# Hybrid encoder block on one Trainium2 core: the first loads in pieces by two queues, idle products ahead of them, and a last store by a second queue

## The chip, the cores and the metric

The kernel runs on one core of one Trainium2 chip. The time is that of one execution in device microseconds; the runs' median is compared. The engines are named as in the profile: PE (TensorE, products; PEld its weight loads), DVE (VectorE), ACT (ScalarE), POOL (GpSimd) and SP (SyncE, which here only issues DMAs). Each engine works through its own list of instructions in order.

## The reference

One layer of a streaming encoder for 512 frames of width 1024, with a memory of 256 frames: RWKV-7 time mixing and an RG-LRU branch side by side, merged by gates, then cross-attention into the memory, then a gated convolutional FFN, each with an RMS norm ahead of it, and a last RMS norm. The change touches the start of the key projection of the memory, which the kernel does first, and the stores of the last norm.

```python
def rms_norm(x, g):
    xf = x.astype(jnp.float32)
    y = xf * lax.rsqrt(jnp.mean(xf * xf, axis=-1, keepdims=True) + NORM_EPS)
    return (y * g.astype(jnp.float32)).astype(x.dtype)

def cross_attention(h, m, w_q, w_kv, w_o):
    ...
    kv = m @ w_kv
    k = kv[..., :D_MODEL].reshape(bsz, -1, X_HEADS, X_HEAD_DIM)
    ...

# in reference():
        x = x + cross_attention(rms_norm(x, norm_x_g[l]), rms_norm(mem, norm_mem_g[l]),
                                w_cq[l], w_ckv[l], w_co[l])
        x = x + conv_ffn(rms_norm(x, norm_ffn_g[l]), w_ffn_in[l], ffn_conv_w[l],
                         ffn_conv_b[l], w_ffn_out[l])
    return rms_norm(x, norm_final_g)
```

## The kernel before

Products keep nearly the precision of float32 by a split: each operand is cut into a rounded part (`hi`, cast by ACT) and the rest (`lo`, a subtraction on DVE), and `mm3` makes three products: hi by hi, hi by lo, lo by hi. So each weight block of 128 by 1024 goes through a load by SP (`wk_r`, L102; four buffers), a cast on ACT (`wk_h`, L114; three buffers), a subtraction on DVE (`wk_l`, L115; three buffers) and 24 products on PE (L160 to L162). `stream` yields these blocks, and `Units` hands them out in eight units of 128 columns.

The first stage computes the keys of the memory, `k_ps`: eight weight blocks `wk`, each by all of the memory. The memory comes as `mraw`, in four quarters of 256 KB (`load_m`), each quarter two of the eight blocks of channels. Each channel block is scaled by the norm's gains and split: `m`, the rounded part on ACT (L281) and the rest on DVE (L282). The gains are 8 of the 240 columns of `pv`, a table of all parameters, loaded in one piece by ACT's queue. Apart from this ACT squares the memory (L284, L286) and DVE adds the squares into `mss` (L287); PE sums `mss` over partitions by a product with `ones` (`rs_ps`, L252, and `rmc_ps`, L294), and from that comes the norm's factor, which multiplies the keys when they leave PSUM (L306). After the keys come the values (`v_ps`), then the input projection (`in_ps`), and all the rest.

The first block of `wk` is loaded in two halves, and `un.fill` puts the loads of the quarters of the memory between them, on SP's queue:

```python
        nc.scalar.dma_start(pv, pv_d)
        load_m(0)
        un = Units(wk_d, "wk")
        un.fill(lambda i: [load_m(q) for q in ((1,), (2, 3))[i]])
```

A scheduler sets the order of the instructions on each engine when the program is built. Calls in `tc.keep_in_program_order` keep the order in which they are written, on their engine; those in `tc.high_priority()` go ahead of others; the rest goes where the scheduler expects it to be ready. Semaphores guard every buffer that is used again.

At the end the last rows of the FFN's output (`fol_ps`) are made in two halves of 256 frames. The second half is normed in two steps of 128 frames. In each step DVE multiplies (L1181) and SP stores (L1183) four channel blocks at a time, two stores of 256 KB a step.

Of the kernel before, what the change touches and what calls it, by code (L numbers as in the profile page):

```python
# [9 lines left out]
F32 = mybir.dt.float32  # L10
F32R = mybir.dt.float32r
AF = mybir.ActivationFunctionType
ALU = mybir.AluOpType
# [4 lines left out]
P = 128  # L18
# [12 lines left out]
IN_RWKV = [12, 13, 4, 5, 0, 1, 8, 9, 6, 7, 2, 3, 10, 11]  # L31
IN_REST = [22, 23, 24, 25, 26, 27, 28, 29, 30, 31, 32, 33, 34, 35, 36, 37, 14, 15, 16, 17, 18, 19, 20, 21]
NEARLY = 3
IN_ORDER = IN_RWKV + IN_REST


# [17 lines left out]
def hybrid_block_kernel(ctx: ExitStack, tc: tile.TileContext, xT_d, mT_d, pv_d, cst_d, win_d, wk_d, wv_d,  # L54
# [18 lines left out]
    def rw_ps(name, pool=None, tag="rw", **kw):  # L73
        return (pool or prw).tile([P, T], F32, tag=tag, name=name, **kw)
# [9 lines left out]
    def par(name, i, n=1):  # L84
        o = PV[name][0]
        return pv[:, o + i:o + i + n]
# [8 lines left out]
    def stream(dram, name, between=None, order=None):  # L95

        for g in order or range(dram.shape[0]):
            with tc.high_priority():
                raw = wp.tile([P, 1024], F32, tag="wr", name=f"{name}_r{g}", bufs=4)
                n = 1024 if between is None else 512  # L100
                for o in range(0, 1024, n):
                    ins = nc.sync.dma_start(raw[:, o:o + n], dram[g, :, o:o + n])  # L102
                    if between is not None:
                        tc.keep_in_program_order(ins)
                        between(o // n)
                    elif len(wdma) == 1:
                        tc.add_manual_dep(ins.ins, wdma[0].ins.name, mybir.DependencyInfo(
                            mybir.DependencyClass.NoSync, mybir.DependencyReason.DATA), reason="order of the loads")
                between = None
                wdma.append(ins)  # L110
                hi = wp.tile([P, 1024], F32R, tag="wh", name=f"{name}_h{g}")
                lo = wp.tile([P, 1024], F32R, tag="wl", name=f"{name}_l{g}")
                for o in range(0, 1024, n):
                    S.copy(hi[:, o:o + n], raw[:, o:o + n])  # L114
                    V.tensor_tensor(lo[:, o:o + n], raw[:, o:o + n], hi[:, o:o + n].bitcast(F32), ALU.subtract)  # L115
            yield hi, lo

    def stream_quarters(srcs, name):
# [81 lines left out]
    def ln_exp_set():  # L200

        return tc.keep_in_program_order(S.preload_act_table_set("natural_log_exp_and_others"))
# [57 lines left out]
    h2 = Split("hT2")  # L260

    with tc.tile_pool(name="p0", bufs=1, reuse_waits="tile") as p0:
        ln_exp_set()
        mraw = p0.tile([P, KB, NMEM], F32, name="mraw")
        xraw = p0.tile([P, KB, T], F32, name="xraw")

        def load_m(q):
            with tc.high_priority():
                tc.keep_in_program_order(
                    nc.sync.dma_start(mraw[:, 2 * q:2 * q + 2, :], mT_d[:, 2 * q:2 * q + 2, :]))  # L270

        nc.scalar.dma_start(pv, pv_d)
        load_m(0)
        un = Units(wk_d, "wk")
        un.fill(lambda i: [load_m(q) for q in ((1,), (2, 3))[i]])
        m2 = p0.tile([P, 2, KB, NMEM], F32R, name="m2")
        mss = p0.tile([P, NMEM], F32, name="mss")
        msq = [p0.tile([P, NMEM], F32, tag="msq", name=f"msq{k}", bufs=2) for k in range(KB)]
        for k in range(KB):
            g = par("nmem", k)  # L280
            S.activation(m2[:, 0, k, :], mraw[:, k, :], AF.Identity, scale=g)  # L281
            V.scalar_tensor_tensor(m2[:, 1, k, :], mraw[:, k, :], g, m2[:, 0, k, :].bitcast(F32),  # L282
                                   ALU.mult, ALU.subtract)
        S.activation(mss, mraw[:, 0, :], AF.Square)  # L284
        for k in range(1, KB):
            S.activation(msq[k], mraw[:, k, :], AF.Square)  # L286
# [878 lines left out]
    for hf in range(2):  # L1165
        ts = slice(hf * 256, (hf + 1) * 256)
        ps = pf.tile([P, T], F32, tag="x", name=f"fol_ps{hf}", bufs=4)
        for kb in range(FB):
            mm3(ps[:, :256], last[kb][0], last[kb][1], g2[kb][:, 0, ts], g2[kb][:, 1, ts], kb == 0, kb == FB - 1)
        step = 128 if hf else 256  # L1170
        for o in range(0, 256, step):
            ts = slice(hf * 256 + o, hf * 256 + o + step)
            sq = ffn_out(ps, KB - 1, ts, slice(o, o + step))
            pss = rw_ps(f"rs_ps{ts.start}", pf, "yz", bufs=4)
            PE.matmul(pss[:, :step], ones, sso[:, ts], start=True, stop=False)
            PE.matmul(pss[:, :step], ones, sq, start=False, stop=True)
            rsqrt(ro[:, ts], pss[:, :step], 1.0 / D, eps[:, 0:1], load=False)
            nb = 4 if hf else 2
            for m in range(0, KB, nb):
                ms = slice(m, m + nb)  # L1180
                V.tensor_tensor(xr[:, ms, ts], xr[:, ms, ts],  # L1181
                                ro[:, ts].unsqueeze(1).to_broadcast([P, nb, step]), ALU.mult)
                nc.sync.dma_start(out_d[:, ms, ts], xr[:, ms, ts])  # L1183


# [75 lines left out]
```

## Time and profile before

| | us |
|---|---|
| runs: all three | 942.82, 942.68, 939.07 |
| median of the runs | 942.68 |
| the profiled execution's own time | 939.86 |
| its span, from the first to the last instruction | 938.1 |
| PE busy | 917.7 (98% of the span) |
| DVE, ACT, POOL busy | 638.2, 468.9, 87.9 |

Times in the profile count from the start of the span. A row of the timeline has the start, the duration, the engine, the line, the operation, the output and inputs with their sizes, and in brackets how long the engine had been idle and what released it. `SPq` and `ACTq` are the issues of DMAs. Two rows of one engine that follow each other closely overlap a little, since the engines are pipelined: what one more instruction costs is read from start to start.

### The profile page before, as it was taken

Reading aid. Unit: us, or ns where it says so; the run is one execution under the profiler, and the core shown is the slowest. Engines: PE = TensorE matmul, PEld = TensorE weight load, DVE = VectorE, ACT = ScalarE, POOL = GpSimd, SP = SyncE. Lnnn points to the kernel's source line nnn. Section 1 sums busy time; section 2 is a strip of 40 time slices with the busy share of each in tenths; the row PEclk is TensorE's granted clock in tenths of the full one; section 3 lists DMA queues with packets and bytes.
Section 4 is the critical chain, followed back from the end, with each engine's and each line's share of the span. In section 5 each row is a group of like instructions: output and inputs, shape, how many; then the busy total and the mean of one; then the engine's idle time right before and its main releaser. Section 6 shows DMA issues by size and latency. Waiting matters only on the chain.

```text
span 938.1 us, 14783 instructions
## 1 busy us (share of the span) xinstructions
PE 917.7 (98%) x5856; PEld 770.4 (82%) x5856; DVE 638.2 (68%) x1043; ACT 468.9 (50%) x711; POOL 87.9 (9%) x101
## 2 busy tenths in 40 slices
PE   7999999999999999999999999999999999999996
PEld 6878776788877767788887778999999999888886
DVE  7784687668845768775566578788878878833333
ACT  7664655522235276434453466666546566532222
POOL 0102121000012200001111111112100000000000
PEclk9999999999999999999999999999999999999998
DMA  8869786464599922658886768999996656422202
GB/s 278 292 242 236 190 214 155 124 162 141 162 228 191 192 40 70 222 175 223 215 234 149 172 140 197 265 267 284 271 270 208 186 183 186 149 90 89 90 23 90
DMA packets 87813, 171.16 MB, mean 182 GB/s; under 512 B 23552, under 2 KB 28800, under 8 KB 87744
## 3 DMA queue, kind: packets, MB, share of 16 engines
q1 hardware_dynamic: 61728, 111.10, 37.7%
q0 software_dynamic: 18688, 47.19, 24.7%
q10 hardware_dynamic: 7328, 11.92, 3.8%
q8 instruction: 46, 0.75, 0.3%
q14 instruction: 23, 0.19, 0.1%
HBM read 158.92 MB, written 57.41 MB: 231 GB/s over the span
## 4 chain that ended last, share of the span: by engine, by line
PE 54%; DMA 3%; DVE 2%; ACT 2%; issue 1%; DVEq 0%; ACTq 0%
PE fo_ps L160 4%; PE fo_ps L161 4%; PE fo_ps L162 4%; PE fx_ps L160 4%; PE fx_ps L161 4%; PE fx_ps L162 4%; PE fyz_ps L161 3%; PE fyz_ps L160 3%; PE fyz_ps L162 3%; DMA wfi_r<-dS 2%; PE co_ps L161 2%; PE q_ps L161 2%; PE mix_ps L162 2%; PE mix_ps L160 2%; PE mix_ps L161 2%; PE q_ps L160 2%
## 5 line engine op out<-in xcount | busy, mean ns | idle before, releaser
L161 PE MATMUL in_ps<-hT,win_h 128*128 128x512 f32 x304 | 124.3, 410 | 0.0
L162 PE MATMUL in_ps<-hT,win_l 128*128 128x512 f32 x304 | 123.0, 405 | 0.0
L160 PE MATMUL in_ps<-hT,win_h 128*128 128x512 f32 x304 | 122.4, 404 | 0.0
L126 ACT CAST wfi_h<-wfi_r 128x1024 fp32r<-128x1024 f32 x77 | 81.0, 1051 | 81.4 <-PE fyz_ps L161 20.7
L127 DVE TENSOR_TENSOR wfi_l<-wfi_r,wfi_h 128x1024 fp32r<-128x1024 f32 x77 | 94.1, 1222 | 38.9 <-ACT wfi_h L126 38.7
L420 POOL DMA_DIRECT2D dS<-in_wfi x66 | 66.6, 1039 | 450.1 <-PE in_ps L160 172.1
L114 ACT CAST win_h<-win_r 128x1024 fp32r<-128x1024 f32 x38 | 39.9, 1049 | 86.7 <-PE in_ps L161 82.4
L115 DVE TENSOR_TENSOR win_l<-win_r,win_h 128x1024 fp32r<-128x1024 f32 x38 | 46.4, 1222 | 49.8 <-ACT win_h L114 49.0
L161 PEld LDWEIGHTS in_ps<-hT,win_h 128*128 128x128 f32 x304 | 57.3, 188 | 16.0 <-issue 2.2
L162 PEld LDWEIGHTS in_ps<-hT,win_l 128*128 128x128 f32 x304 | 57.3, 188 | 15.5 <-issue 2.0
L160 PEld LDWEIGHTS in_ps<-hT,win_h 128*128 128x128 f32 x304 | 57.1, 188 | 15.3 <-issue 1.4
L115 DVE TENSOR_TENSOR wfo_l<-wfo_r,wfo_h 128x1024 fp32r<-128x1024 f32 x22 | 26.9, 1225 | 52.1 <-ACT wfo_h L114 52.1
L114 ACT CAST wfo_h<-wfo_r 128x1024 fp32r<-128x1024 f32 x22 | 23.1, 1049 | 62.0 <-PE fo_ps L161 61.3
L160 PE MATMUL fx_ps<-hq,wfi_h 128*128 128x256 f32 x176 | 50.0, 284 | 2.1 <-ACT sn L1093 2.0
L161 PE MATMUL fx_ps<-hr,wfi_h 128*128 128x256 f32 x176 | 49.7, 282 | 0.0
L162 PE MATMUL fx_ps<-hr,wfi_l 128*128 128x256 f32 x176 | 49.6, 282 | 0.0
L160 PE MATMUL fx_ps<-hr,wfi_h 128*128 128x256 f32 x176 | 49.5, 281 | 0.0
L160 PE MATMUL fyz_ps<-hq,wfi_h 128*128 128x256 f32 x176 | 49.2, 280 | 0.0
L161 PE MATMUL fx_ps<-hq,wfi_h 128*128 128x256 f32 x176 | 49.2, 279 | 0.0
L161 PE MATMUL fyz_ps<-hq,wfi_h 128*128 128x256 f32 x176 | 49.1, 279 | 0.0
L162 PE MATMUL fx_ps<-hq,wfi_l 128*128 128x256 f32 x176 | 49.1, 279 | 0.0
L162 PE MATMUL fyz_ps<-hq,wfi_l 128*128 128x256 f32 x176 | 49.1, 279 | 0.0
(421 smaller groups left out, 2513.7 us busy)
## 6 DMA issues: line engine op xcount, KB each, us to landing
dS<-in_wfi POOLq DMA_DIRECT2D x66, 512.0 KB, 8.2
wfi_r<-dS SPq DMA_DIRECT2D x44, 512.0 KB, 6.4
win_r<-in_win SPq DMA_DIRECT2D x38, 512.0 KB, 4.7
wfi_r<-in_wfi SPq DMA_DIRECT2D x33, 512.0 KB, 5.3
dS<-dS POOLq DMA_DIRECT2D x22, 512.0 KB, 5.8
wfo_r<-in_wfo SPq DMA_DIRECT2D x22, 512.0 KB, 3.5
wv_r<-in_wv SPq DMA_DIRECT2D x8, 512.0 KB, 5.3
dG<-gs ACTq DMA_DIRECT2D x16, 256.0 KB, 2.1
```

The lines of the kernel that those rows point to most:

```text
L114: S.copy(hi[:, o:o + n], raw[:, o:o + n])
L115: V.tensor_tensor(lo[:, o:o + n], raw[:, o:o + n], hi[:, o:o + n].bitcast(F32), ALU.subtract)
L126: S.copy(hi, raw)
L127: V.tensor_tensor(lo, raw, hi.bitcast(F32), ALU.subtract)
L160: first = PE.matmul(ps, lh, rh, start=start, stop=False, **kw)
L161: PE.matmul(ps, lh, rl, start=False, stop=False, **kw)
L162: PE.matmul(ps, ll, rh, start=False, stop=stop, **kw)
L420: return lambda: nc.gpsimd.dma_start(s(out), src, **kw)
```

## The change

In the first stage: the first block of `wk` is loaded in four pieces of 256 columns instead of two of 512; the first quarter of the memory stays on SP's queue, and the other three go to ACT's, behind a load of the 8 columns of gains; the rest of `pv` is loaded by two more issues on ACT, kept in order behind the last copy of the memory. ACT's table load stands behind its first four issues. The casts, copies and subtractions of the first block and of the memory are kept in a written order (piece, two channel blocks, piece, two channel blocks, and so on). Nine products of `ones` by `ones` into a PSUM tile that nobody reads (`wake`) go first on PE. At the end, the last of the four stores of the last half goes to ACT's queue.

```diff
+NWAKE = 9
...
-                n = 1024 if between is None else 512
+                n = 1024 if between is None else 256
                 for o in range(0, 1024, n):
                     ins = nc.sync.dma_start(raw[:, o:o + n], dram[g, :, o:o + n])
                     if between is not None:
                         tc.keep_in_program_order(ins)
-                        between(o // n)
...
-                    S.copy(hi[:, o:o + n], raw[:, o:o + n])
-                    V.tensor_tensor(lo[:, o:o + n], raw[:, o:o + n], hi[:, o:o + n].bitcast(F32), ALU.subtract)
+                    a = S.copy(hi[:, o:o + n], raw[:, o:o + n])
+                    b = V.tensor_tensor(lo[:, o:o + n], raw[:, o:o + n], hi[:, o:o + n].bitcast(F32), ALU.subtract)
+                    if between is not None:
+                        tc.keep_in_program_order(a)
+                        tc.keep_in_program_order(b)
+                        between(o // n)
+                between = None
...
+        o, w = PV["nmem"]
+        with tc.high_priority():
+            tc.keep_in_program_order(nc.scalar.dma_start(pv[:, o:o + w], pv_d[:, o:o + w]))
+
         def load_m(q):
             with tc.high_priority():
+                tc.keep_in_program_order((nc.scalar if q else nc.sync).dma_start(
+                    mraw[:, 2 * q:2 * q + 2, :], mT_d[:, 2 * q:2 * q + 2, :]))
+
+        for q in range(KB // 2):
+            load_m(q)
+        ln_exp_set()
+        m2 = p0.tile([P, 2, KB, NMEM], F32R, name="m2")
+
+        def split_m(q):
+            for k in (2 * q, 2 * q + 1):
+                g = par("nmem", k)
                 tc.keep_in_program_order(
-                    nc.sync.dma_start(mraw[:, 2 * q:2 * q + 2, :], mT_d[:, 2 * q:2 * q + 2, :]))
-
-        nc.scalar.dma_start(pv, pv_d)
-        load_m(0)
+                    S.activation(m2[:, 0, k, :], mraw[:, k, :], AF.Identity, scale=g))
+                tc.keep_in_program_order(
+                    V.scalar_tensor_tensor(m2[:, 1, k, :], mraw[:, k, :], g, m2[:, 0, k, :].bitcast(F32),
+                                           ALU.mult, ALU.subtract))
+
         un = Units(wk_d, "wk")
-        un.fill(lambda i: [load_m(q) for q in ((1,), (2, 3))[i]])
+        un.fill(split_m)
+        for sl in (slice(0, o), slice(o + w, NPV)):
+            tc.keep_in_program_order(nc.scalar.dma_start(pv[:, sl], pv_d[:, sl]))
+        wake = rw_ps("wake")
+        with tc.high_priority():
+            for i in range(NWAKE):
+                PE.matmul(wake[:, 0:P], ones, ones, start=True, stop=True)
...
+        queues = [nc.sync, nc.scalar]
...
-                nc.sync.dma_start(out_d[:, ms, ts], xr[:, ms, ts])
+                q = queues[m // nb % 2] if ts.stop == T else nc.sync
+                q.dma_start(out_d[:, ms, ts], xr[:, ms, ts])
```

The scheduler orders the first stage anew; from the input projection on the order is the same but for that last store. Three places in the built programs matter. In the names the numbers are those of buffers; the weight blocks one to six are, before, `wk_r` 97, 202, 236, 270, 304 and 339, and now 101, 220, 254, 288, 322 and 357.

First, ACT's list from its start. Before:

```order
L202 ACT_TABLE_LOAD
L272 DMA pv<-in_pv 128x240
L284 ACTIVATE mss<-mraw 128x256
L286 ACTIVATE msq_112<-mraw 128x256
L114 CAST wk_h_103<-wk_r_97 128x512
L281 ACTIVATE m_109<-mraw,pv 128x256 x3
L114 CAST wk_h_103<-wk_r_97 128x512
L281 ACTIVATE m_109<-mraw,pv 128x256 x3
L286 ACTIVATE msq_113<-mraw 128x256
L286 ACTIVATE msq_114<-mraw 128x256
L114 CAST wk_h_204<-wk_r_202 128x1024
```

Now, from its fourth row on (the rows ahead are the four issues and the table load):

```order
L113 CAST wk_h_106<-wk_r_101 128x256
L289 ACTIVATE m_100<-mraw,pv 128x256 x2
L113 CAST wk_h_106<-wk_r_101 128x256
L289 ACTIVATE m_100<-mraw,pv 128x256 x2
L113 CAST wk_h_222<-wk_r_220 128x1024
L113 CAST wk_h_106<-wk_r_101 128x256
L304 ACTIVATE mss<-mraw 128x256
L113 CAST wk_h_256<-wk_r_254 128x1024
L306 ACTIVATE msq_146<-mraw 128x256
L289 ACTIVATE m_100<-mraw,pv 128x256
```

The cast of the second block now stands ahead of the last two pieces of the first block and of the second half of the memory; the squares of the memory have moved behind it.

Second, DVE's list around the last addition into `mss`. Before (`msq_118` is the last square, and block five's subtraction comes seven rows later):

```order
L115 TENSOR_TENSOR wk_l_239<-wk_r_236,wk_h_238 128x1024
L287 TENSOR_TENSOR mss<-mss,msq_116 128x256
L115 TENSOR_TENSOR wk_l_273<-wk_r_270,wk_h_272 128x1024
L287 TENSOR_TENSOR mss<-mss,msq_117 128x256
L366 TENSOR_TENSOR dp<-dp,pv 128x4
L376 TENSOR_SCALAR dp<-dp 128x4
L287 TENSOR_TENSOR mss<-mss,msq_118 128x256
```

Now (`msq_152` is the last square; ahead of these rows stand seven operations on parameters, from `pv`, and ahead of those the other additions):

```order
L114 TENSOR_TENSOR wk_l_291<-wk_r_288,wk_h_290 128x1024
L114 TENSOR_TENSOR wk_l_325<-wk_r_322,wk_h_324 128x1024
L114 TENSOR_TENSOR wk_l_360<-wk_r_357,wk_h_359 128x1024
L307 TENSOR_TENSOR mss<-mss,msq_152 128x256
L381 TENSOR_TENSOR dp<-dp 128x4
```

The last addition stood behind the subtractions of blocks three and four and now stands behind those of blocks four, five and six. ACT's list has the casts of blocks four and five ahead of the last square, and the cast of block six behind it.

Third, PE's list at `rs_ps`. Before (`k_ps_235` is the product of the third block):

```order
L160 MATMUL k_ps_235<-m_109,wk_h_238 128x256
L161 MATMUL k_ps_235<-m_109,wk_h_238 128x256
L162 MATMUL k_ps_235<-m_109,wk_l_239 128x256
L252 MATMUL rs_ps<-mss,ones 128x256
L294 MATMUL rmc_ps<-ones,mss 128x1 x2
L160 MATMUL k_ps_235<-m_109,wk_h_238 128x256
L161 MATMUL k_ps_235<-m_109,wk_h_238 128x256
```

Now (`k_ps_253` is the product of the third block, `k_ps_287` that of the fourth):

```order
L164 MATMUL k_ps_253<-m_100,wk_h_256 128x256
L165 MATMUL k_ps_253<-m_100,wk_h_256 128x256
L166 MATMUL k_ps_253<-m_100,wk_l_257 128x256
L256 MATMUL rs_ps<-mss,ones 128x256
L314 MATMUL rmc_ps<-ones,mss 128x1 x2
L164 MATMUL k_ps_287<-m_100,wk_h_290 128x256
L165 MATMUL k_ps_287<-m_100,wk_h_290 128x256
```

Before, 60 of the 72 products of the first three blocks stood ahead of `rs_ps`; now all 72 do.

More of the change, by code (lines that the diff above doesn't have):

```diff
@@ L108, in stream @@
                             mybir.DependencyClass.NoSync, mybir.DependencyReason.DATA), reason="order of the loads")
-                between = None
                 wdma.append(ins)
@@ L262, in hybrid_block_kernel @@
     with tc.tile_pool(name="p0", bufs=1, reuse_waits="tile") as p0:
-        ln_exp_set()
         mraw = p0.tile([P, KB, NMEM], F32, name="mraw")
         xraw = p0.tile([P, KB, T], F32, name="xraw")
+        o, w = PV["nmem"]
+        with tc.high_priority():
+            tc.keep_in_program_order(nc.scalar.dma_start(pv[:, o:o + w], pv_d[:, o:o + w]))
         def load_m(q):
             with tc.high_priority():
+                tc.keep_in_program_order((nc.scalar if q else nc.sync).dma_start(
[7 more added lines that the diff above has]
+                g = par("nmem", k)
                 tc.keep_in_program_order(
-                    nc.sync.dma_start(mraw[:, 2 * q:2 * q + 2, :], mT_d[:, 2 * q:2 * q + 2, :]))
-        nc.scalar.dma_start(pv, pv_d)
-        load_m(0)
+                    S.activation(m2[:, 0, k, :], mraw[:, k, :], AF.Identity, scale=g))
+                tc.keep_in_program_order(
+                    V.scalar_tensor_tensor(m2[:, 1, k, :], mraw[:, k, :], g, m2[:, 0, k, :].bitcast(F32),
+                                           ALU.mult, ALU.subtract))
         un = Units(wk_d, "wk")
-        un.fill(lambda i: [load_m(q) for q in ((1,), (2, 3))[i]])
-        m2 = p0.tile([P, 2, KB, NMEM], F32R, name="m2")
+        un.fill(split_m)
[5 more added lines that the diff above has]
+                PE.matmul(wake[:, 0:P], ones, ones, start=True, stop=True)
         mss = p0.tile([P, NMEM], F32, name="mss")
         msq = [p0.tile([P, NMEM], F32, tag="msq", name=f"msq{k}", bufs=2) for k in range(KB)]
[L279 to L283, printed above, removed]
         S.activation(mss, mraw[:, 0, :], AF.Square)
```

## The prediction, made before the changed kernel ran

> **What bounds the kernel now.** I read the page first, then PE's waits in the chain-of-waits view, then the timeline of the first 20 us and of the last 10, since the change lies there alone.
>
> ```profile
> span 938.1 us, 14783 instructions
> PE 917.7 (98%) x5856; PEld 770.4 (82%) x5856; DVE 638.2 (68%) x1043; ACT 468.9 (50%) x711; POOL 87.9 (9%) x101
> ```
>
> PE's waits (what waited for whom: us in total, times, longest):
>
> ```profile
> PE k_ps L160 <- ACT m L281: 6.3, 1, 6.3
> PE ss L524 <- ACT sq L522: 2.3, 1, 2.3
> PE fx_ps L160 <- ACT sn L1093: 2.0, 2, 1.7
> PE k_ps L162 <- DVE wk_l L115: 0.4, 1, 0.4
> ```
>
> PE is the bound: of some 20 us without a product, 6.3 are the start. The later waits (ss, fx_ps) hang on ACT work that hangs on PE itself, so a shift of PE's stream at 20 us moves everything behind it by as much. Two things count: when PE reaches its even pace, and the last stores.
>
> ```profile
> 0.74 1.28 ACT L202 ACT_TABLE_LOAD   x1 [0.74 <-PEq L1250]
> 0.77 0.40 ACTq L272 DMA_DIRECT2D pv<-in_pv  x1
> 5.18 0.62 ACT L114 CAST wk_h<-wk_r 128x512 fp32r<-128x512 f32 x1 [0.47 <-DMA wk_r<-in_wk]
> 6.27 0.58 PE L160 MATMUL k_ps<-m,wk_h 128*128 128x256 f32 x1 [6.27 <-ACT m L281]
> 7.57 0.41 PE L160 MATMUL k_ps<-m,wk_h 128*128 128x256 f32 x1
> 7.78 0.41 PE L161 MATMUL k_ps<-m,wk_h 128*128 128x256 f32 x1
> ...
> 12.11 0.28 PE L161 MATMUL k_ps<-m,wk_h 128*128 128x256 f32 x1
> 12.22 0.28 PE L162 MATMUL k_ps<-m,wk_l 128*128 128x256 f32 x1
> ...
> 16.52 0.70 PE L252 MATMUL rs_ps<-mss,ones 128*128 128x256 f32 x2
> ```
>
> Products of 256 columns start 0.21 apart at 7.6 us and 0.117 apart from 12 us: PE begins at half speed. The landmark is rs_ps (the sum of squares of mem, L252) at 16.52: by the order of instructions 60 of the 72 products of the first three weight blocks stand ahead of it, and it waits for nothing, as the last addition into mss is early on DVE.
>
> **The change part by part.** In the new order rs_ps stands behind all 72 products, and the last addition into mss stands on DVE behind the splits of weight blocks four, five and six. Those splits reuse the buffers (three each of wk_h and wk_l) of blocks one, two and three, so they cannot start before PE has read these. PE's queue is in order: at rs_ps it waits for work that itself waits for PE. That wait is new, and block four's products, queued behind rs_ps, wait with it. Its price needs these rows:
>
> ```profile
> 3.99 0.42 ACT L284 ACTIVATE mss<-mraw 128x256 f32<-128x256 f32 x1 [1.97 <-DMA mraw<-in_mT]
> 4.31 0.40 ACT L286 ACTIVATE msq<-mraw 128x256 f32<-128x256 f32 x1
> 9.25 1.03 ACT L114 CAST wk_h<-wk_r 128x1024 fp32r<-128x1024 f32 x1
> 10.19 0.91 ACT L281 ACTIVATE m<-mraw,pv 128x256 fp32r<-128x256 f32 x2
> ...
> 5.09 0.17 DVE L349 TENSOR_SCALAR dp<-pv 128x14 f32<-128x14 f32 x1
> 5.16 0.16 DVE L353 TENSOR_SCALAR dp<-pv 128x4 f32<-128x4 f32 x1
> 6.44 1.27 DVE L282 SCALAR_TENSOR_TENSOR m<-mraw,pv,m 128x256 fp32r<-128x256 f32 x3
> 7.63 0.69 DVE L115 TENSOR_TENSOR wk_l<-wk_r,wk_h 128x512 fp32r<-128x512 f32 x1
> 12.90 1.22 DVE L115 TENSOR_TENSOR wk_l<-wk_r,wk_h 128x1024 fp32r<-128x1024 f32 x1
> 14.04 0.42 DVE L287 TENSOR_TENSOR mss<-mss,msq 128x256 f32<-128x256 f32 x1
> 14.37 1.22 DVE L115 TENSOR_TENSOR wk_l<-wk_r,wk_h 128x1024 fp32r<-128x1024 f32 x1
> ```
>
> From start to start: on ACT a square 0.32, a block cast 0.94, a scaled copy of mem 0.41; on DVE a block subtraction 1.14, an addition into mss 0.33, a mem subtraction 0.40 (7.63 less 6.44, by three), a parameter operation 0.08. For a piece of 256 columns I take 0.32 on ACT and 0.33 on DVE, like the other 256-column rows. The loads:
>
> ```profile
> 3.08 0.43 SPq L102 DMA_DIRECT2D wk_r<-in_wk  x1
> wk_r<-in_wk SPq DMA_DIRECT2D x1, 512.0 KB, 5.5
> pv<-in_pv ACTq DMA_DIRECT2D x1, 120.0 KB, 3.7
> GB/s 0 0 116 210 342 296 369 391 391 393 350 374 407 410 415 426 191 87 382 208 158 268 306 186 262 289 300 279 328 317 180 371 371 322 382 344 311 328 371 415
> ```
>
> The last row cuts the first 30 us into 40 slices. *Second block's landing.* It was issued at 3.08 and landed at 8.58, with itself 1912 KB moved (three quarters of mem 768, block one 512, parameters 120, itself 512). Now all of mem may go ahead: 1024 + 512 + 4 + 512 = 2052 KB. The 140 KB more at 390 GB/s are 0.36, so 8.9. If SP's queue were served alone it would be 1280 KB, 632 less, about 7.0. I take 8.9: two queues with work share the engines, as pv's load shows, which came from ACT's queue and landed at 4.5, between mem's first load (by the row of 3.99 above) and block one's half (5.16, by the cast above). ACT has by then done two pieces and four copies of mem and stands still, since this cast is next in its order; behind it wait the last two pieces and the other half of mem, which have landed. So smaller, earlier pieces are lost to the order.
>
> *Up to the last product of block one.* ACT's cast ends at 9.95. DVE then has, in order, two block subtractions (2.28), two pieces (0.66), four mem subtractions (1.60) and four additions (1.32): 5.86, so 15.8. ACT's own list (two casts, two pieces, five squares, four copies, 5.8 from 8.9) ends at 14.7 and keeps ahead. PE finishes with block one's buffer at about 16.3.
>
> *From there to rs_ps, two ways.* By ACT: casts of blocks four and five, a square, cast six (0.94 + 0.94 + 0.32 + 1.04) end at 19.6; DVE's subtraction of block six and the last addition (1.22 + 0.42) give 21.3. By DVE: the rest of the parameters is loaded late, by ACT's queue behind its last copy of mem, issued at about 14.3 and 14.7; with 3.7 us, as pv took above, it lands at 18.4; seven parameter operations, three block subtractions and the addition (0.56 + 3.42 + 0.42) give 22.8. With the 2.3 of the quickest store further down it would be 17.0, and 21.4. I take 21.9, between the two. PE's remaining 16 products from 16.3 end at 18.2: some 3.7 us idle at rs_ps.
>
> *The shift.* rs_ps at 21.9 instead of 16.52, less the twelve products of 0.117 that now stand ahead of it (1.4): **+4.0**. Ends: block two at 7.4 (ACT is not free sooner) and quick parameters, +2.0; late parameters, +4.9.
>
> *The clock.*
>
> ```profile
> 150.77:154.19 3.42, 1.10 (x6) 0.58 (x4) 1.55 (x4) 0.78 (x2) 0.00 (x0) 1.00 0.60 205
> 154.19:157.60 3.41, 3.41 (x6) 2.00 (x7) 2.52 (x4) 3.36 (x6) 0.00 (x0) 0.50 0.14 20
> 607.40:610.80 3.40, 1.66 (x15) 1.45 (x14) 3.22 (x6) 3.40 (x7) 0.00 (x0) 1.00 0.86 222
> ```
>
> Second column: PE busy; the column third from the end: granted clock. A stretch of 3.4 us with 1.10 busy (the ss wait of 2.3) was followed by 3.41 us at 0.50, that is 1.7 lost; one with 1.66 busy was itself granted 1.00. A gap of 3.7 at rs_ps leaves most placings of such a stretch under 1.1 busy, so a half-speed stretch follows it: 1.7, taken as **+1.4** since part may fall into the gap (ends 0 and 1.7). PE also idles for most of 8.1 to 11.2 (waits for block two's cast and subtraction), which may leave it at half speed to 14; DVE sets the pace there, so **+0.4** (0 to 0.9). The Trainium skill, "TensorE: Matmul & The Clock Gate" (Part 1), has the default clock return after an idle window of about 3.4 us; a gap without one such window would by it cost nothing more. The trace differs: 2.32 us of idling sufficed here.
>
> *Idle products.* Nine on the constant fill PE from about 1.0, where it has nothing to do: cost nothing. Their gain is bounded by the half-speed start, 18 products by 0.095, 1.7; but PE next waits for block two whatever its clock, so I take 0 for the landmark. *ACT's four issues* ahead of its table load (4 x 0.45) let that end at about 3.85 instead of 2.02, before the first piece lands (about 4.6): nothing. SP has fewer issues; POOL's order is unchanged.
>
> *The last stores.*
>
> ```profile
> 932.87 0.60 DVE xr L1181
> 932.90 0.40 SPq L1183 DMA_DIRECT2D out<-xr  x1
> 933.56 0.43 SPq L1183 DMA_DIRECT2D out<-xr  x1
> out<-xr SPq DMA_DIRECT2D x1, 256.0 KB, 2.3
> out<-xr SPq DMA_DIRECT2D x1, 256.0 KB, 3.0
> out<-xr SPq DMA_DIRECT2D x1, 256.0 KB, 3.6
> ```
>
> Only the fourth store moves to ACT's queue. It was issued 0.09 after DVE's last multiplication (933.47), with SP free since 933.30: nothing to gain at the issue. The third landed at 935.9, the fourth at 937.2, though issued 0.66 apart: transfers set the end. **-0.1** (from -0.6, the spacing of the landings less that of the issues, to +0.2 if ACT issues later than SP would). The Trainium skill, "Trainium Kernel Development and Optimization" (Key Constraints), says the same of a second queue: it saves issue time alone, as all queues run on the same 16 engines.
>
> **Sum.** The profiled execution took 939.86 (span 938.1). 939.86 + 4.0 + 1.4 + 0.4 - 0.1 = 945.6. The runs shown lie at 939.1 and at 942.7 to 942.8; the profiled one is of the lower level, the median of the upper, 2.8 above. I cannot tell which level the next median falls on and add half, 1.4: **947.0**.
>
> **The rivals.** (1) The other side: the idle products and the early pieces do what their place suggests. PE would start at 5.9 rather than 6.27, run at full speed (1.7) and skip the wait of 0.4 for wk_l: -2.5, and 938.7 on the same footing (939.86 + 1.4 - 2.5 - 0.1). It decides if the last addition into mss is done by 18.2, when the 72 products are; it would have to come 3.7 us sooner, so block two at about 5.2, when some 1 MB has moved by the GB/s row and it needs 1.3. With the waits on buffers, which no load shortens, I see little for it: 0.08. (2) The order costs what I say but the clock does not drop: 945.2, the case of the skill's rule on a full idle window; 0.22. (3) SP's queue is served first, block two is there when ACT is: shift 2.0, clock 1.4, so 944.6; 0.15. (4) Parameters late and both stretches at half speed: 4.9 + 1.7 + 0.9, so 948.7; 0.15. My forecast: 0.40.
>
> **How the numbers follow.** The two levels put 1.4 about each case. Below 941.5 lies most of (1) and little else, above 950.5 a part of (4): range 941.5 to 950.5. My own case alone: 945.0 to 949.0. A measurement of this kernel tells about 0.5% (4.7 us) from no change. Runs side by side share their levels, so the effect counts: my case (+5.7) and (4) exceed it, (2) and (3) (+3.9, +3.3) do not. That is 0.55 for slower, of which I give 0.02 away for the levels; faster by 4.7 is beyond even (1) unless the levels help: 0.05.
>
> **What would show it.**
>
> ```profile
> 56.80 0.40 PE L160 MATMUL in_ps<-hT,win_h 128*128 128x512 f32 x1
> ```
>
> In the changed kernel's trace: wake from 1.0 to about 5; the second block's cast at 8.9 and PE idle before it; the 72nd product at about 18; PE idle more than 3 us at rs_ps, released by DVE's mss; a granted clock of 0.5 in the stretch behind it; this first product of the input projection later by 4 to 6.5; the last store landing as long after its issue as now. Wrong would be: mss ready when PE gets there, or the second block landing near 5.

## The result, and the profile after

| | before | changed |
|---|---|---|
| median of six runs, us | 940.21 (939.02 to 942.82) | 948.84 (946.60 to 953.06) |
| ratio, 95% interval | | 1.0094 (1.0068 to 1.0119) |
| profiled execution, its span | 939.86, 938.1 | 951.43, 949.7 |

The change costs 8.6 us. PE's busy time grew by 8.7 (from 917.7) though only nine products were added: these took 4.2 (1.06 to 5.27), and products at half speed count as longer. The page, and PE's waits (us in total, times, longest):

```profile
PE 926.4 (98%) x5874; PEld 778.1 (82%) x5874; DVE 639.0 (67%) x1045; ACT 468.7 (49%) x713; POOL 87.9 (9%) x101
```

```profile
PE rs_ps L256 <- DVE mss L307: 5.4, 1, 5.4
PE k_ps L164 <- ACT wk_h L113: 2.8, 1, 2.8
PE fx_ps L164 <- ACT sn L1113: 1.9, 3, 1.2
PE k_ps L164 <- ACT m L289: 1.2, 1, 1.2
```

Two waits are new: 2.8 for the cast of the second weight block, and 5.4 at `rs_ps` for the last addition into `mss`. The start wait shrank from 6.3 to 1.2 only because idle products fill it. The timeline of the same stretch, PE's rows first, then ACT's, then DVE's:

```profile
6.42 0.58 PE L164 MATMUL k_ps<-m,wk_h 128*128 128x256 f32 x1 [1.15 <-ACT m L289]
12.44 0.39 PE L164 MATMUL k_ps<-m,wk_h 128*128 128x256 f32 x1 [2.79 <-ACT wk_h L113]
27.56 1.22 PE L256 MATMUL rs_ps<-mss,ones 128*128 128x256 f32 x2 [5.38 <-DVE mss L307]
68.69 0.40 PE L164 MATMUL in_ps<-hT,win_h 128*128 128x512 f32 x1
...
11.35 1.35 ACT L113 CAST wk_h<-wk_r 128x1024 fp32r<-128x1024 f32 x2 [3.48 <-DMA wk_r<-in_wk]
20.21 2.00 ACT L113 CAST wk_h<-wk_r 128x1024 fp32r<-128x1024 f32 x2 [2.08 <-PE k_ps L165]
...
12.42 2.79 DVE L114 TENSOR_TENSOR wk_l<-wk_r,wk_h 128x1024 fp32r<-128x1024 f32 x3 [4.01 <-ACT wk_h L113]
17.59 0.87 DVE L291 SCALAR_TENSOR_TENSOR m<-mraw,pv,m 128x256 fp32r<-128x256 f32 x2
23.16 0.17 DVE L369 TENSOR_SCALAR dp<-pv 128x14 f32<-128x14 f32 x1 [3.82 <-DMA pv<-in_pv]
23.68 3.49 DVE L114 TENSOR_TENSOR wk_l<-wk_r,wk_h 128x1024 fp32r<-128x1024 f32 x3
27.09 0.42 DVE L307 TENSOR_TENSOR mss<-mss,msq 128x256 f32<-128x256 f32 x1
```

Read backwards from 27.56: the last addition starts at 27.09, behind three block subtractions, behind the parameters (landed 23.1). ACT's casts of blocks four and five had begun at 20.21, when PE freed the buffers. PE was late in part because the second block's cast began at 11.35 instead of 9.25, with ACT idle for 3.5 ahead of it and half of mem and two pieces queued behind; e5 shows that half speed on PE does it too. PE's speed over this stretch (columns as in the prediction):

```profile
20.20:23.60 3.40, 1.98 (x17) 1.77 (x16) 0.45 (x6) 3.37 (x5) 0.00 (x0) 1.00 0.94 358
23.60:27.00 3.40, 0.00 (x0) 0.00 (x0) 3.40 (x6) 2.31 (x3) 0.00 (x0) 1.00 0.37 116
27.00:30.40 3.40, 2.84 (x11) 2.66 (x12) 2.51 (x13) 1.41 (x5) 0.00 (x0) 0.50 0.96 319
30.40:33.80 3.40, 3.40 (x18) 3.40 (x18) 2.47 (x8) 0.86 (x3) 0.00 (x0) 0.50 0.98 358
```

After the wait the clock is at half for two stretches of 3.4 us. PE was busy for 6.2 of them, so about 3.1 us are lost, not 1.7.

### The profile page after: what moved, and what is told of

Its sections match the earlier page's. It is cut to its first block, busy times and chain, and to the rows that moved or that the text cites. A ratio compares the mean times of both kernels' runs of the same rounds, so it can differ in the third digit from the quotient of the medians.

```text
span 949.7 us, 14827 instructions
## 1 busy us (share of the span) xinstructions
PE 926.4 (98%) x5874; PEld 778.1 (82%) x5874; DVE 639.0 (67%) x1045; ACT 468.7 (49%) x713; POOL 87.9 (9%) x101
## 3 DMA queue, kind: packets, MB, share of 16 engines
q0 software_dynamic: 18688, 47.19, 24.4%
## 4 chain that ended last, share of the span: by engine, by line
PE 49%; DMA 5%; DVE 3%; ACT 3%; issue 1%; DVEq 0%; ACTq 0%
PE fo_ps L165 4%; PE fo_ps L164 4%; PE fo_ps L166 4%; DMA wfi_r<-dS 3%; PE fx_ps L164 3%; PE fx_ps L166 3%; PE fx_ps L165 3%; PE fyz_ps L164 2%; PE fyz_ps L165 2%; PE fyz_ps L166 2%; PE co_ps L165 2%; PE mix_ps L164 2%; PE mix_ps L165 2%; PE co_ps L164 2%; PE mix_ps L166 2%; PE co_ps L166 2%
## 5 line engine op out<-in xcount | busy, mean ns | idle before, releaser
L130 ACT CAST wfi_h<-wfi_r 128x1024 fp32r<-128x1024 f32 x77 | 81.1, 1053 | 84.2 <-PE fx_ps L165 24.8
```

The costliest lines, as they stand in the source:

```text
L130: S.copy(hi, raw)
```

## The experiments

The first products of three stages, and each kernel's time against the kernel before on the same chip. All starts are from one profile each; executions of one kernel differ by some us, also further on.

| kernel | rs_ps | v_ps | in_ps | ratio, 95% interval |
|---|---|---|---|---|
| before | 16.5 | 32.9 | 56.8 | |
| changed | 27.6 | 45.4 | 68.7 | 1.0094 (1.0068 to 1.0119) |
| e5, changed again | 24.8 | 42.8 | 66.0 | 1.0097 (1.0074 to 1.0120) |
| e1, last store alone | 16.4 | 33.2 | 57.0 | 0.9987 (0.9968 to 1.0005) |
| e2, idle products alone | 16.7 | 33.1 | 57.7 | 1.0002 (0.9981 to 1.0024) |
| e3, squares in order | 19.1 | 38.5 | 61.8 | 1.0052 (1.0032 to 1.0072) |
| e4, parameters early | 21.1 | 38.3 | 61.5 | 1.0072 (1.0051 to 1.0094) |
| e6, as e3, no idle products | 19.4 | 38.7 | 61.9 | 1.0043 (1.0027 to 1.0060) |
| e7, parameters first | 19.8 | 37.1 | 60.3 | 1.0056 (1.0033 to 1.0078) |
| e8, before, third buffer for pr | 17.1 | 34.3 | 57.9 | 1.0004 (0.9980 to 1.0027) |
| e9, parameters behind | 23.5 | 41.3 | 64.6 | 1.0090 (1.0056 to 1.0125) |
| e10, fill the wait | 23.6 | 38.5 | 61.8 | 1.0075 (1.0046 to 1.0104) |
| e11, second block behind | 18.4 | 35.8 | 59.1 | 1.0025 (1.0001 to 1.0048) |
| e12, longer rows | 25.0 | 41.6 | 64.8 | 1.0090 (1.0059 to 1.0122) |

**e1.** The last store alone, on the kernel before:

```diff
+        queues = [nc.sync, nc.scalar]
...
-                nc.sync.dma_start(out_d[:, ms, ts], xr[:, ms, ts])
+                q = queues[m // nb % 2] if ts.stop == T else nc.sync
+                q.dma_start(out_d[:, ms, ts], xr[:, ms, ts])
```

> The kernel before with only the last of its four stores moved to ACT's queue; everything else as before. My theory (the transfers set the end, not the issues): within 0.1 us of the kernel before, the last store lands about 4.3 us after its issue as before (932.90 + 0.66 to 937.2). Rival (two queues overlap, so the 0.66 between the issues goes): 0.6 us sooner at the end of the span. Either way no part of the +8.6 us of the whole change comes from here; if this kernel is slower by more than 2 us, my account of the start is wrong.

No difference that can be told: the interval, -3.0 to +0.5 us, holds my theory and the rival's 0.6, so the trace has to speak. The moved store landed 3.6 after its issue, as the fourth did before (the 4.3 in my expectation was counted from the third store's issue), and its issue came when DVE was done:

```profile
out<-xr SPq DMA_DIRECT2D x3, 256.0 KB, 2.6
out<-xr ACTq DMA_DIRECT2D x1, 256.0 KB, 3.6
```

**e2.** The idle products alone, on the kernel before:

```diff
+        wake = rw_ps("wake")
+        with tc.high_priority():
+            for i in range(9):
+                PE.matmul(wake[:, 0:P], ones, ones, start=True, stop=True)
```

> The kernel before with only the nine idle products of ones by ones ahead on PE; loads and orders as before. My theory: the first key products run at full clock (0.117 instead of 0.21 apart), rs_ps comes up to 1.0 us sooner than its 16.5, since DVE's subtractions pace this stretch, and little of that reaches the end, because the later wait at ss hangs on a store and not on PE: 0 to -1.0 us. Rival one (the gain is kept): -1.7 us. Rival two (the idle products bring the clock down later or delay the first product): +0.5 us or more. If it is slower by over 3 us, idle products and not the order are the cost of the change.

No difference that can be told (the interval is -1.8 to +2.3 us). Contrary to what I expected, the first key products were not faster: they start 0.21 apart up to 10.1, as in the kernel before up to 10.8. In this execution idle products from 1.06 to 5.27 did not bring the clock up for the work behind them; in others they did (see the last section).

**e3.** The changed kernel, with the squares and additions in the pinned order:

```diff
+                tc.keep_in_program_order(S.activation(msq[k] if k else mss, mraw[:, k, :], AF.Square))
+                if k:
+                    tc.keep_in_program_order(V.tensor_tensor(mss, mss, msq[k], ALU.add))
```

> The changed kernel, but the squares of mem and the additions into mss are written into the same pinned order as the copies, so that the last addition stands on DVE ahead of the subtractions of blocks four to six, and rs_ps on PE behind 60 key products instead of 72. The late rest of the parameters and the late second block stay. My theory (three causes in a row: late second block, order, late parameters): the wait of 5.4 at rs_ps is gone, but PE then waits for block four's lower part, which stands on DVE behind the parameters that land at 23; a wait of 3 to 5 at k_ps in its place, PE resumes about 25 instead of 27.6, so 2 to 4 us sooner than the changed kernel (945 to 947). Rival one (the order alone): no wait over 1 us after rs_ps, 5 to 8 us sooner (941 to 944). Rival two (the loads alone): the wait moves but keeps its 5.4, no gain (949).

The wait at `rs_ps` is gone and `in_ps` comes 4 to 7 sooner than in the two profiles of the changed kernel. The two waits that matter in what is left of the stage:

```profile
PE k_ps L164 <- ACT wk_h L113: 2.5, 1, 2.5
PE k_ps L166 <- DVE wk_l L114: 1.8, 2, 1.5
```

The second is block four's lower part, behind the parameters (21.2), 1.5 and not the 3 to 5 I expected. By the ratios (1.0052 against 1.0094 and 1.0097) the order is about half of the loss; with it right, some 5 us remain.

**e4.** The changed kernel, with the rest of the parameters behind the memory:

```diff
         for q in range(KB // 2):
             load_m(q)
+        for sl in (slice(0, o), slice(o + w, NPV)):
+            with tc.high_priority():
+                tc.keep_in_program_order(nc.scalar.dma_start(pv[:, sl], pv_d[:, sl]))
         ln_exp_set()
```

> The changed kernel, but the rest of the parameters is issued on ACT's queue directly behind the memory, ahead of the table load, instead of behind the last copy of mem. The scheduler then also puts the last addition into mss ahead of the subtractions of blocks four to six (rs_ps behind 66 key products). My theory: no wait at rs_ps and none on parameters; what is left is the late second block (it landed at 11.3), a little later still by the 116 KB ahead of it (0.3 us); PE then runs through, in_ps comes 2 to 5 us later than in the kernel before (56.8) instead of 11.9, and the time is 942 to 945. Rival one (the clock's half speed is the cost and comes by the first gap anyway): 945 to 947. Rival two (late loads in general): as the changed kernel, 949.

My theory failed on the time: 948.4, not 942 to 945, which is rival two's number, but not by late loads in general. The wait at `rs_ps` went, as expected, but two things came in its place. ACT stood ahead of its two new issues until 5.60, when the first memory load of its queue had landed (1.19 + 4.4), so that its table load and its first cast came some 2 us later: PE's wait of 3.3. And the scheduler put the parameter operations at the head of DVE's list, and DVE stood for them until 9.9, ahead of its first splits: PE's wait of 2.4. ACT's and DVE's rows, and PE's waits:

```profile
5.60 0.82 ACTq L284 DMA_DIRECT2D pv<-in_pv  x2
6.45 1.28 ACT L206 ACT_TABLE_LOAD   x1 [6.45 <-DMA mraw<-in_mT]
9.88 0.17 DVE L370 TENSOR_SCALAR dp<-pv 128x14 f32<-128x14 f32 x1 [8.82 <-DMA pv<-in_pv]
```

```profile
PE k_ps L164 <- ACT m L292: 3.3, 1, 3.3
PE k_ps L165 <- DVE m L294: 2.4, 1, 2.4
```

**e5.** The changed kernel again, without an edit.

> The changed kernel as it is, for a second profile and more times, since the wait at ss and the landing of the second block differ from one execution to the next. My theory: the median stays 7 to 9 us above the kernel before; the second block lands between 9.5 and 11.5 (9.7 in the two runs with the same first loads, 11.3 in the first profile of this kernel), and wherever it lands, PE waits 4 us or more at rs_ps for DVE's last addition into mss. Rival (the late second block of 11.3 was the cause): with a landing near 9.7 the wait at rs_ps falls under 3 us and in_ps starts less than 65 instead of 68.7.

The same loss with another split. The second block's cast began at 10.03 and the parameters had landed by 20.07; still PE waited 3.0 at `rs_ps`, and `in_ps` came at 66.0. That is below the 4 that I had set and only just outside what the rival asked for (under 3, under 65): the wait is there without the late landing, but 2.4 shorter:

```profile
11.13 0.58 PE L164 MATMUL k_ps<-m,wk_h 128*128 128x256 f32 x1 [1.61 <-ACT wk_h L113]
24.82 1.22 PE L256 MATMUL rs_ps<-mss,ones 128*128 128x256 f32 x2 [3.03 <-DVE mss L307]
...
10.03 1.35 ACT L113 CAST wk_h<-wk_r 128x1024 fp32r<-128x1024 f32 x2 [2.12 <-DMA wk_r<-in_wk]
19.84 2.00 ACT L113 CAST wk_h<-wk_r 128x1024 fp32r<-128x1024 f32 x2 [3.03 <-PE k_ps L165]
...
16.28 0.88 DVE L291 SCALAR_TENSOR_TENSOR m<-mraw,pv,m 128x256 fp32r<-128x256 f32 x2
20.07 0.18 DVE L369 TENSOR_SCALAR dp<-pv 128x14 f32<-128x14 f32 x1 [2.05 <-DMA pv<-in_pv]
20.93 3.50 DVE L114 TENSOR_TENSOR wk_l<-wk_r,wk_h 128x1024 fp32r<-128x1024 f32 x3 [0.25 <-ACT wk_h L113]
```

Here DVE waited for ACT's cast, and that for PE. PE freed the buffer only 2.7 after DVE's last split of mem (17.16 to 19.84), as it ran at half speed until 17.7 (17 products in a stretch, 28 in the next):

```profile
10.00:13.40 3.40, 1.81 (x6) 1.52 (x7) 2.29 (x3) 3.37 (x7) 0.00 (x0) 0.50 0.58 187
13.40:16.80 3.40, 3.40 (x17) 3.40 (x17) 3.40 (x10) 3.23 (x9) 0.00 (x0) 0.50 0.62 193
16.80:20.20 3.40, 3.40 (x28) 3.40 (x27) 1.25 (x5) 0.37 (x2) 0.00 (x0) 0.88 1.04 355
```

**e6.** As e3, with `NWAKE = 0`:

```diff
-NWAKE = 9
+NWAKE = 0
```

> As the run with the squares and additions in the pinned order, but without the nine idle products. There the granted clock was full from 4.4, when PE had nothing else to do, and half from 7.8 to 14.6, with 17 products 0.21 apart after the second block had come. Theory one (idle products bring the clock up too soon and it falls back while the loads are waited for): without them full clock from about 10 to 11, the products from there on 0.117 apart, rs_ps up to 1.5 us sooner than 19.1, and the time 1 to 2 us less than with them (944 to 945). Theory two (DVE and ACT set the pace there, the clock costs nothing): no difference (946). If idle products help at all, this run is slower: 947 or more.

The times do not tell the two apart (1.0043 against 1.0052, the intervals overlap) and the starts are within 0.3. Without idle products the products also start 0.21 apart until 15.4, so theory one falls: behind the wait for the second block PE runs at half speed, with idle products or without. In the kernel before PE works through from 7.4 to 10.8 and is at full speed from there. That this one wait keeps the clock down is argued and not shown: in e11, where it is 0.3, PE has several shorter gaps in the first block and runs at half speed from 14.3 to 17.0 all the same.

**e7.** The changed kernel, with all parameters in one load at the head of ACT's queue:

```diff
-            tc.keep_in_program_order(nc.scalar.dma_start(pv[:, o:o + w], pv_d[:, o:o + w]))
+            tc.keep_in_program_order(nc.scalar.dma_start(pv, pv_d))
...
-        for sl in (slice(0, o), slice(o + w, NPV)):
-            tc.keep_in_program_order(nc.scalar.dma_start(pv[:, sl], pv_d[:, sl]))
```

> The changed kernel, but all of the parameters are loaded in one piece first on ACT's queue (120 KB, as in the kernel before), ahead of the memory, instead of 8 columns first and the rest later. The scheduler then puts the last addition into mss ahead of blocks four to six. With the rest directly behind the memory DVE stood until 10.9 for it, ahead of its first splits, and the first two waits of PE were 3.3 and 2.4. My theory (a parameter wait on DVE's in-order list, wherever it is put, moves all of the stage): first key product at about 6.6, no wait on parameters, in_ps 2 to 3.5 later than before, time 943 to 945. Rival (two queues and small pieces themselves delay the loads): 946 to 948, with the second block at 10 or later.

Neither the order at `rs_ps` nor the parameters hold anything up now, and `in_ps` is 3.5 late; the time, 945.9, lies between what my theory and what the rival expected. What stands out is the pinned cast of the second block, for which ACT stands still; PE's wait for it is 2.2 (e11 takes it away):

```profile
9.93 1.04 ACT L113 CAST wk_h<-wk_r 128x1024 fp32r<-128x1024 f32 x1 [1.90 <-DMA wk_r<-in_wk]
```

**e8.** The kernel before, with `bufs=3` for the two tiles of tag `pr`:

```diff
-            prs[j] = pp.tile([P, T], F32, tag="pr", name=f"pr{j}", bufs=2)
+            prs[j] = pp.tile([P, T], F32, tag="pr", name=f"pr{j}", bufs=3)
```

> The kernel before with one edit that the change does not have: three buffers instead of two for pr, so that DVE's next pr need not wait until a store of the one before has landed (4.0 in the profile of before, 1.1 in that with the last store alone; the wait of 2.3 at ss and 1.7 of half speed hang on it). My theory (this store's landing, which differs between executions, is most of why ss was late in one profile and not in the others, and why my sum took the later stages as moving along one for one): no wait on the store, no wait at ss, median 1 to 3 us less than before, and less spread than 938 to 946. Rival (the spread comes from elsewhere: scores, FFN): no difference, within 0.5 us.

The wait on the store and that at ss are gone in its profile, yet no gain can be told (-1.9 to +2.5 us): most of my theory's 1 to 3 us is excluded, and the result is as the rival has it. In e1, which still has two buffers, the wait on the store was 1.1 (4.0 in the profile of before) and ss was not waited for. From DVE's waits in e1 between 100 and 165 us:

```profile
DVE pr L480 <- DMA dBo<-pr: 1.1, 1, 1.1
```

The executions differ elsewhere too. In e8 PE lost more in the FFN, between 580 and 815 us, where in the profile of before only 2.0 was lost, under code that is the same. Its largest wait there:

```profile
PE fx_ps L160 <- ACT sn L1093: 4.4, 4, 1.6
```

From the first product of `fx_ps` to that of `fo_ps` it took 229.5 in e8 and 222.3 before.

**e9.** The changed kernel, with the parameter operations ordered behind the last addition:

```diff
+            tc.add_manual_dep(ins.ins, last.ins.name, mybir.DependencyInfo(
+                mybir.DependencyClass.NoSync, mybir.DependencyReason.DATA), reason="behind mss")
```

> The changed kernel with one dependency more: the operations on the late parameters stand on DVE behind the last addition into mss instead of ahead of the subtractions of blocks four to six; every other order is as in the changed kernel. In its two profiles the parameters landed at 23.1 and at 20.1, and ACT's casts of blocks four and five (which wait for PE to free their buffers) began at 20.2 and at 19.8. My theory (two ways to rs_ps side by side, the later one counts, and they lie close together): rs_ps at about 25 whenever the parameters land, a gain of 0 to 2.5 us, about 1 in the median (948 to 949). Rival one (the parameters are the cause): rs_ps at 22 or sooner, 3 us or more gained. Rival two: none gained, the same wait of 3 to 5 with ACT's cast as the one that DVE waits for.

No gain in the time, and a wait of 3.0 at `rs_ps` as in e5, with DVE waiting for ACT's cast alone (18.51, released by PE): nearest to rival two. (`rs_ps` came at 23.5, sooner than the 25 expected: the second block's cast began at 9.52 and PE's half speed ended at 16.0, against 10.03 and 17.7 in e5.) So the late parameters bind in some executions (the first profile, where DVE waited for them until 23.16 and ACT's first cast was done by about 21.2) and then only for what they exceed the other way; they are not a cost on top.

**e10.** The changed kernel, with idle products directly ahead of `rs_ps`:

```diff
+        for i in range(10):
+            PE.matmul(wake[:, 0:P], ones, msq[KB - 1][:, 0:P], start=True, stop=True)
```

> The changed kernel with ten more idle products of 128 by 128 on PE directly ahead of rs_ps, which wait only for the last square of mem (ACT, about 22) and so keep PE busy in the second half of its wait there; all other orders are as in the changed kernel. They move no work sooner. Theory (the half-speed clock of 6.8 us behind the wait is a cost of its own): granted clock stays 1.00 behind rs_ps, v_ps and in_ps come 2.5 to 3.4 us sooner than in the changed kernel for the same rs_ps, 945.5 to 947.5. Rival (the stretch behind rs_ps is paced by DVE and ACT, and half speed costs nothing): no difference from the changed kernel, 948.5 to 950.

The trace bears the theory out. PE's rows, and its speed:

```profile
20.76 2.50 PE L309 MATMUL wake<-msq,ones 128*128 128x128 f32 x20 [0.42 <-ACT msq L306]
23.55 0.70 PE L256 MATMUL rs_ps<-mss,ones 128*128 128x256 f32 x2 [0.30 <-DVE mss L307]
38.54 0.39 PE L164 MATMUL v_ps<-wv_h,m 128*128 128x512 f32 x1
```

```profile
20.40:23.60 3.20, 2.55 (x21) 2.36 (x21) 3.20 (x7) 3.17 (x5) 0.00 (x0) 1.00 0.79 251
23.60:27.00 3.40, 3.40 (x28) 3.35 (x29) 3.14 (x13) 2.66 (x8) 0.00 (x0) 1.00 0.89 308
27.00:30.40 3.40, 3.40 (x32) 3.40 (x31) 3.14 (x10) 1.12 (x2) 0.00 (x0) 1.00 0.87 325
```

`rs_ps` came no sooner than in e9, but `v_ps` followed it by 15.0 instead of 17.8 (and `in_ps` came at 61.8 instead of 64.6): 2.8 for the clock. The time points the same way (1.0075 against 1.0097 and 1.0090), with intervals that overlap, and lies just above my bounds.

**e11.** As e7, with the cast and subtraction of the second block in the pinned order behind the first block's:

```diff
-                    if between is not None:
+                    if between is not None or len(wdma) == 2:
                         tc.keep_in_program_order(a)
                         tc.keep_in_program_order(b)
...
         un.fill(split_m)
+        un.ahead.append(next(un.it))
```

> The kernel with all parameters loaded first, and with the cast and the subtraction of the second weight block kept in order behind all pieces of the first block and all copies of mem, instead of ahead of the last two pieces. Theory (the pinned early cast makes ACT stand still, but ACT's and DVE's work up to the last addition into mss is the same, so another order only moves the wait): PE's wait for the second block's cast shrinks from 2.2 and first-block products fill it, but the last addition stands behind the subtractions of blocks two to four, rs_ps comes at 18.5 to 19.5 behind only 48 products, and in_ps is again 2.5 to 4 later than in the kernel before: 944 to 946. Rival (the cast's place was the whole rest of the loss): in_ps within 1 of the kernel before, 940 to 942.

944.15, as expected; the wait for the second block is 0.3 and ACT does not stand still, but `rs_ps` comes at 18.4 behind 48 products, and `in_ps` is 2.3 late, both just under what I expected. It has the lowest ratio of the kernels with the new loads, and is still slower than before, at the edge of what the interval (1.0001 to 1.0048) can tell. What makes up these last 2.3 was not taken apart.

**e12.** The changed kernel, with longer rows in the first loads:

```diff
-            tc.keep_in_program_order(nc.scalar.dma_start(pv[:, o:o + w], pv_d[:, o:o + w]))
+            gm = cp.tile([P, 128], F32, name="gm")
+            tc.keep_in_program_order(nc.scalar.dma_start(gm, pv_d[:, o + w - 128:o + w]))
...
-                for o in range(0, 1024, n):
-                    ins = nc.sync.dma_start(raw[:, o:o + n], dram[g, :, o:o + n])
+                for o in range(0, 1024, max(n, 512)):
+                    ins = nc.sync.dma_start(raw[:, o:o + max(n, 512)], dram[g, :, o:o + max(n, 512)])
...
-                g = par("nmem", k)
+                g = gm[:, 128 - w + k:128 - w + k + 1]
```

> The changed kernel, but its first loads have longer rows: the first weight block in two loads of 512 columns (cast in four pieces as in the change), and the gains as part of a load of 128 columns into a tile of their own instead of 8 columns. In the first 4 us the changed kernel moved 0.38 MB against 0.57 in the kernel before, with 148 packets under 512 bytes against 35, and its second block's cast began at 9.65 to 11.35 in six profiles with these loads, against 8.6 to 9.9 in four with the old loads. Theory (small packets delay all that is queued behind them): 0.5 MB or more in the first 4 us, the cast at 9.4 or sooner, 1 to 2 us less than the changed kernel (947 to 948). Rival (two queues at once delay the second block, whatever the rows): the cast at 9.7 or later, time as the changed kernel.

In the four profiles with the old loads the cast began at 9.2 to 10.0, and not at the 8.6 to 9.9 that I had noted. Here it began at 9.35, as my theory asked, but hardly sooner than in e9 and e10 (9.52, 9.39); only 0.43 MB moved in the first 4 us, and the time is that of the changed kernel. So longer rows did not make the first 4 us faster. That the new loads are slower at first is plain. GB/s over the first 12 us in 40 slices, before and then changed:

```profile
GB/s 0 0 0 0 0 27 171 181 248 187 316 379 300 273 328 389 369 369 389 382 389 376 416 423 355 335 348 423 355 348 403 423 396 410 410 396 423 437 437 410
```

```profile
GB/s 1 0 0 0 0 27 178 187 149 187 155 189 148 209 329 386 376 393 399 403 406 386 410 369 358 256 314 382 341 273 328 314 273 314 410 437 396 246 150 137
```

From 2.4 to 4.2 us the old loads move up to 379, the new 148 to 209. Whether two queues or the order of the loads does this was not tried apart and stays open.

The second block's lateness has another source, which the traces show: its load is issued later. SP's rows in the changed kernel, and the time from issue to landing of mem's first quarter and of the second block:

```profile
0.74 0.40 SPq L277 DMA_DIRECT2D mraw<-in_mT  x1
1.19 1.37 SPq L103 DMA_DIRECT2D wk_r<-in_wk  x3
4.93 0.33 SPq L103 DMA_DIRECT2D wk_r<-in_wk  x1
5.30 0.43 SPq L103 DMA_DIRECT2D wk_r<-in_wk  x1
```

```profile
mraw<-in_mT SPq DMA_DIRECT2D x1, 256.0 KB, 4.0
wk_r<-in_wk SPq DMA_DIRECT2D x1, 512.0 KB, 6.0
```

Three pieces follow mem's first quarter, and then SP stands. With ACT's four loads eight are under way. The fourth piece is issued at 4.93, 0.2 after mem's first quarter landed (0.74 + 4.0), and it is so in all nine profiles of kernels with four pieces. In the first 26 us of each of the fourteen profiles at most eight loads are under way over both queues; what sets this limit is not shown. The second block's load was the seventh before, issued at 3.08. Now it is the tenth, issued at 5.30, and in e5 at 4.38: that is 2.2 and 1.3 of the 2.8 and 1.4 by which it landed later than before (11.3 and 10.0 against 8.6). In e12, with two loads for the first block, it was the eighth, issued at 2.17, but took 7.2 to land.

## Why the prediction came out as it did

The time, 948.84, is 1.8 above the predicted 947.0 and in the range; the effect, 8.6, is larger than the 5.7 forecast. The mechanism held, but that the number came so close is in part luck: the shift and the clock behind `rs_ps` were put at 5.4 together and measured 12.4 in the first profile and 9.7 in e5, while 1.4 was added for levels that do not exist and 4.0 of waiting and half speed at ss were carried over from the profile of before, which the changed kernel did not have. By steps:

- *The order puts rs_ps behind work that waits for PE: right*, and shown by e3. The chain's own lengths held too: from ACT's cast of block four to `rs_ps` 5.0 was forecast and 4.98 measured in e5 (there DVE's three subtractions behind the first cast fill it, and not ACT's three casts as forecast); from the parameters' landing 4.4, and 4.4 in the first profile (23.13 to 27.56).
- *The shift of +4.0 was mis-sized*: 9.6 in the first profile (27.56 less 16.52 less 1.4) and 6.9 in e5. Three inputs failed. The second block was put at 8.9 from the bytes ahead of it, and its cast began at 11.35 and 10.03. The bytes were not the error: by 8.9 the changed kernel had moved 2.1 MB (239 GB/s on average), as much as the sum counts. But the sum left the issue of the load where it was, and it came 2.2 and 1.3 later (e12). "SP has fewer issues" does not hold for those ahead of this load: five before and five now, and over both queues six before and nine now. PE was to free block one's buffers 0.5 after DVE's last split of mem; it took 1.7 (18.46 to 20.21) and 2.7, at half speed. The parameters were to be issued at about 14.3 and to land at 18.4 with the 3.7 that the load took before; the first of their two loads was issued at 16.3 and took 6.8, to 23.1, and in e5 it was issued at 15.0 and took 5.0, to 20.1.
- *The clock in the first gap, +0.4, was mis-sized in kind.* I reasoned that DVE sets the pace there. But PE's pace decides when the buffers come free, and with them ACT's next casts: the half speed lies on the path, inside the shift above.
- *The clock behind rs_ps, +1.4*: half speed came as forecast and lasted two stretches, not one; 2.8 by e10. In e5 an idle time of 3.03 sufficed; by the Trainium skill, "TensorE: Matmul & The Clock Gate" (Part 1), it takes an idle window of about 3.4. The trace decides here as it did for the 2.32 of before.
- *Last store -0.1 and idle products 0*: nothing measured speaks against them (e1, e2), but the times tell apart no less than some 2 us; that transfers set the last store's end is borne out by its landing (3.6 from either queue). The faster first block, from which the idle products' bound came, was not there in e2.
- *"A shift of PE's stream moves everything behind it by as much": half right.* The +11.9 at `in_ps` was +8.0 by 296 us, since the wait at ss and its half speed (2.3 + 1.7), which the profile of before has, did not come; the cross-attention added 2.1 (10.1 at its end) and the FFN 1.6. These vary between executions with the same code.
- *Two levels, +1.4*: none are to be seen. The 72 runs of before beside e1 to e12 spread without a gap from 935.5 to 945.9, with medians of 940.4 to 941.7.

Of the rivals, (3), the second block there when ACT is, is excluded by the casts; (2), no clock drop, by the windows; (4), late parameters with both stretches at half speed, 948.7, names what bound in the first profile, but its shift, 4.9, is half of the 9.6 measured, so that its number meets the median is luck; in e5 the parameters did not bind.

None of the kernels run beats the kernel before: e1, e2 and e8 are level with it. Taken in turn, the order and the parameters (e7, 1.0056) and the place of the second block's cast (e11, 1.0025) account for most of the 1.0094, with intervals of 0.2% to each.

## What to carry to other kernels

Loads in smaller pieces brought nothing here, neither with a later, larger load's work ahead of the pieces in an in-order engine's list (e7) nor with that work put behind (e11): look in the built order for the first instruction that stands still, and for what has landed behind it. More loads can also push the issue of the next large one back: count the loads ahead of it over all queues, and read when it is issued, not only when it lands. A wait for work whose buffers the waiting engine itself must free cost the wait, the slow clock behind it, and the slowness of the work that was to free them. A profile of one execution holds waits that the next has not: take each term from a wait that has a reason in the order, and check a second profile before counting on the others.

## What the runs showed that I had not expected

The clock does not come back as soon as work does. In the changed kernel it stayed at 0.50 for two stretches of 3.4 us, of which PE was busy for 2.84 in the first and all of the second, and was full behind that; in e5 the same at 24.4 to 31.2. So a stretch that is 84% busy did not bring it up here, and a full one did. In e12 the clock fell at 25.6, 0.6 after PE had resumed behind a wait of 4.4, PE was busy for all of that stretch, and it alone was at half. This agrees with the busy window of about 3.4 us in the Trainium skill, "TensorE: Matmul & The Clock Gate" (Part 1). Nine idle products ahead of the first work, over 4.2 us, left the work behind them at half speed in some executions (e2 and the changed kernel's first, products 0.21 apart) and not in others (e3 and e9, 0.12 apart from 7.2 and 7.0); why is not shown, and no gain in the time can be told (e2, e6). Ten of them in the middle of a wait (e10) were worth 2.8 us on PE.
